# Recurrent layers of a four-layer encoder: channel tiles of 126 instead of 112, whole and halved gate blocks, gates of four tiles together

## The chip, the cores and the metric

One Trainium2 chip (trn2), of which one core is used. The kernel is one launch that runs a whole encoder trunk over 256 time steps. The metric is the device time of one execution in microseconds (us). Times are given as the median of three runs; the trace is of one further, profiled execution.

The engines have short names: PE is TensorE (PEld is its weight load, which overlaps it), DVE is VectorE, ACT is ScalarE, POOL is GpSimd, SP is SyncE, which here issues nearly all DMA transfers.

## The reference

Four layers of three sub-layers each: a token mixer, a cross-attention into 256 memory tokens, a squared-ReLU MLP, each followed by a layer norm. The mixers are, in order, recurrent, RWKV, chunked attention, recurrent. Only the recurrent mixer (layers 0 and 3) is touched. With 1344 channels in 16 blocks of 84:

```python
u = x @ w_in                                       # 256 x 1024 by 1024 x 2688
gate_branch = gelu(u[..., :1344])
xr = causal_depthwise_conv(u[..., 1344:], conv_w, conv_b)      # 4 taps
xb = xr.reshape(bsz, seq, 16, 84)
gates = einsum('bsnc,gncd->bsgnd', xb, gate_w) + gate_b        # two gates, block-diagonal
r, i = sigmoid(gates)
log_a = -8 * r * softplus(-lam)
a = exp(log_a)
b = sqrt(-expm1(2 * log_a)) * (i * xr)
h[t] = a[t] * h[t-1] + b[t]                        # along time, per channel
out = (h * gate_branch) @ w_out                    # 1344 x 1024
```

All of it is fp32.

## The kernel before

**Weights.** A large product is done three times, since each fp32 operand is split into a high part and a low remainder: `mm_piece` issues for each 128-row slice of a weight the matmuls high by high, low by high and high by low (L272, L273, L274). The weights come in a stream of chunks of two such slices: SP issues the load of a chunk into one of 4 buffers `wraw` (L105), ACT casts it to `whi` (L454), DVE forms `wlo` (L455), and after that `wlo` SP may issue the load that takes the buffer over, four chunks later. The splits run up to 7 chunks ahead of PE. All engines work through their instructions in the order in which the kernel writes them, and SP through its issues, so what stands ahead in a queue delays what stands behind it.

**The recurrent layer** (`lru`) holds its 1344 channels in 12 tiles of 112. Three tiles are four blocks of 84, so the gate products of three tiles (a *group*, `g`) are closed in themselves; a block that straddles two tiles makes 7 products of tile by tile (`GPAIRS`) for each gate. The steps stand in this order:

- `x_piece(0..2)`: the recurrent half of `w_in`, 448 columns each, and behind it, half a piece later, `conv(i)`: PE transposes to channels by time (L801), ACT scales (L807), DVE adds three taps (L811).
- `load_gw`: four loads of gate weights (343 KB, two groups) on SP's queue ahead of the remaining weight chunks, and the other four on ACT's queue, behind the sigmoids of groups 0 and 1 (L834). In layer 3 the two `mem_load` transfers (`kT`) follow them, in layer 0 they come after `x_piece(2)`.
- `gates(0)`, `conv(2)`, `gates(1)`, `gates(2)`, `gates(3)`: 14 fp32 matmuls of 256 columns a group (L847; each shows as two records), three times two sigmoids with a bias from `par` (L850, L851) and a tanh (L852), 256 wide, and one DVE product by the gate `i` (L853).
- `g_piece(0)` and `g_piece(1)`: the gelu half of `w_in`. Between their row halves stand `decay` (Exp, Square on ACT, L862, L864; DVE L865) and `scan` (Sqrt L868; DVE product L869 and a scan along time L871) of the four groups. The casts and the `wlo` of the next weight chunks stand in the same ACT and DVE queues, behind them. Exp, Square, Tanh and Sigmoid, Sqrt, and Gelu need ACT table loads when they change.
- In layer 0 `mem_split` (cast and remainder of `kT`: `memhi`, `memlo`), then `g_piece(2)` and the memory product L313, which fills PE between the groups of the last step.
- For each group PE transposes the gelu branch (L931), DVE multiplies (L934), and the result is split. `out_gemm` multiplies by `w_out`: 12 tiles by 2 column halves by 2 row halves by 3, 144 matmuls of 512 columns.

Of the kernel before, what the change touches and what calls it, by code (L numbers as in the profile page):

```python
# [16 lines left out]
T = 256  # L17
# [3 lines left out]
CT = 112  # L21
NT = DR // CT
GPAIRS = [(0, 0), (1, 0), (0, 1), (1, 1), (2, 1), (1, 2), (2, 2)]
# [42 lines left out]
class Stream:  # L66
# [46 lines left out]
    def _split(self):  # L113
        if self.ns >= len(self.plan):
            return
        k, i = self.k, self.ns
        while self.nd <= i:
            self._dma()
        _, _, p, f, whole = self.plan[i]
        raw = self.raw.pop(i)  # L120
        if whole:
            self.hl[i] = raw
            self.ns += 1
            return
        hi = k.hl_p.tile([128, 1024], F32R, name="whi", tag="whi")
        lo = k.hl_p.tile([128, 1024], F32R, name="wlo", tag="wlo")
        for c in self._cols(i, f):
            k.split(raw[:p, c], hi[:p, c], lo[:p, c])
        self.hl[i] = (hi, lo)
        self.ns += 1  # L130
        self._dma()
# [31 lines left out]
    def done(self, i):  # L163
# [9 lines left out]
        while self.ns < end and self.ns < i + self.hl_bufs:  # L173
            if any(self.plan[q][4] for q in range(i + 1, self.ns + 1)) and self.nd <= self.ns:
                break
            self._split()

# [54 lines left out]
class Kern:  # L232
# [20 lines left out]
    def mm_piece(self, acc, chunks, lhs, p, w, kpc=2, kt0=0, start=True, stop=True, last=False, near=None):  # L253
# [4 lines left out]
        for ci, c in enumerate(chunks):  # L258
            if not self.dry:
                wh, wl = self.st.hl[c]  # L260
                for k in range(kpc):
# [5 lines left out]
                    kt = kt0 + ci * kpc + k  # L267
                    a, b = lhs(kt)
                    ws = slice(k * w, (k + 1) * w)
# [393 lines left out]
    def out_gemm(self, name, idx, n, lhs, p):  # L663

        for nh in range(2):
            a = [self.acc(), self.acc()]
            parts = [range(n)] if n <= 4 else [range(n // 2), range(n // 2, n)]
            for part in parts:
                end = part is parts[-1]
                ch = [self.st.take(name, (*idx, nh, q), p, 1024) for q in part]  # L670
                last = end and nh == 1
                near = self.room(ch, self.next_ht()) if last else None
                for t in range(2):
                    self.mm_piece(a[t], ch, lhs[t], p, 512, kt0=2 * part[0], start=part[0] == 0, stop=end,
                                  last=t == 1 and not last, near=near if t else None)
# [104 lines left out]
    def lru(self, l, j):  # L780
        nc, tc = self.nc, self.tc
        with tc.tile_pool(name="lru", bufs=1, reuse_waits="tile") as p:
            par, cc = self.par[:, j], self.cc[:, j]
            gn = [p.tile([128, DR], F32, name=f"gn{t}") for t in range(2)]
            xc = [p.tile([CT, 3, T], F32, name="xc", tag="A", bufs=4) for _ in range(4)]
            nat = {}

            def x_piece(i):
                for t, a in self.gemm("lru_in", (j, 3 + i), 4, self.hT, 128, 448):
                    s = gn[t][:, 896:] if i == 2 else p.tile([128, 448], F32, name="xn", tag="CB"[i], bufs=4)  # L790
                    nc.scalar.copy(s, a[:, :448])
                    nat[i, t] = s
                    if i and t == 0:
                        conv(i - 1)

            def conv(i):
                for b in range(2):
                    ps = self.tp()
                    for q in range(2):
                        for t in range(2):  # L800
                            nc.tensor.transpose(ps[:CT, q * T + t * 128:q * T + t * 128 + 128],  # L801
                                                nat[i, t][:, (2 * b + q) * CT:(2 * b + q + 1) * CT], self.ident)
                    xy = []
                    for q in range(2):
                        c = 4 * i + 2 * b + q
                        x, y = ps[:CT, q * T:(q + 1) * T], xc[c // 3][:, c % 3, :]
                        nc.scalar.activation(y, x, AF.Identity, bias=par[:, c, 4:5], scale=par[:, c, 3:4])  # L807
                        xy.append((c, x, y))
                    for s in range(1, 4):
                        for c, x, y in xy:  # L810
                            nc.vector.scalar_tensor_tensor(  # L811
                                out=y[:, s:], in0=x[:, :T - s], scalar=par[:, c, 3 - s:4 - s], in1=y[:, s:],
                                op0=ALU.mult, op1=ALU.add)

            def g_piece(i, between=lambda t: None):
                accs = []
                for t, a in self.gemm("lru_in", (j, i), 4, self.hT, 128, 448):
# [4 lines left out]
            def gelu(i, accs):  # L822
                for t in range(2):
                    nc.scalar.activation(gn[t][:, i * 448:(i + 1) * 448], accs[t][:, :448], AF.Gelu_apprx_tanh)

            ra, th = [], []

            gws = []

            def load_gw(g, queue):  # L830
                gws.append([])
                for gate in range(2):
                    w = p.tile([CT, 7, CT], F32, name="gw", tag="gw", bufs=4)
                    queue.dma_start(w, self.I["lru_gw"][j, g, gate])  # L834
                    gws[g].append(w)

            def gates(g):
                gw = gws[g]
                r = p.tile([CT, 3, T], F32, name="ra", tag="B", bufs=4)
                h = p.tile([CT, 3, T], F32, name="th", tag="C", bufs=4)  # L840
                it = p.tile([CT, 3, T], F32, name="it", tag="tmp", bufs=2)
                for o in range(3):
                    ps = self.acc() if LV & 8 else self.mm()
                    ks = [(n, k) for n, (k, oo) in enumerate(GPAIRS) if oo == o]
                    for gate in range(2):
                        for n, k in ks:
                            nc.tensor.matmul(ps[:CT, gate * T:(gate + 1) * T], lhsT=gw[gate][:, n, :], rhs=xc[g][:, k, :],  # L847
                                             start=n == ks[0][0], stop=n == ks[-1][0])
                    c = 3 * g + o
                    nc.scalar.activation(r[:, o, :], ps[:CT, :T], AF.Sigmoid, bias=par[:, c, 6:7])  # L850
                    nc.scalar.activation(it[:, o, :], ps[:CT, T:], AF.Sigmoid, bias=par[:, c, 7:8])  # L851
                    nc.scalar.activation(h[:, o, :], r[:, o, :], AF.Tanh, scale=cc[:, c:c + 1])  # L852
                nc.vector.tensor_tensor(out=xc[g], in0=xc[g], in1=it, op=ALU.mult)  # L853
                ra.append(r)
                th.append(h)
                if g < 2:
                    load_gw(g + 2, nc.scalar)

            def decay(g):
                for o in range(3):  # L860
                    c = 3 * g + o
                    nc.scalar.activation(ra[g][:, o, :], ra[g][:, o, :], AF.Exp, scale=cc[:, c:c + 1])  # L862
                a2 = p.tile([CT, 3, T], F32, name="a2", tag="tmp", bufs=2)
                nc.scalar.activation(a2, ra[g], AF.Square)  # L864
                nc.vector.scalar_tensor_tensor(out=th[g], in0=a2, scalar=1.0, in1=th[g], op0=ALU.add, op1=ALU.mult)  # L865

            def scan(g):
                nc.scalar.activation(th[g], th[g], AF.Sqrt, scale=-1.0)  # L868
                nc.vector.tensor_tensor(out=th[g], in0=th[g], in1=xc[g], op=ALU.mult)  # L869
                for o in range(3):  # L870
                    nc.vector.tensor_tensor_scan(xc[g][:, o, :], ra[g][:, o, :], th[g][:, o, :], 0.0, ALU.mult, ALU.add)  # L871

            x_piece(0)
            for g in range(2):
# [6 lines left out]
            V = LV  # L881
            if V & 1:
                gates(0)
# [3 lines left out]
            if not V & 1:  # L887
                gates(0)
            if V & 2:
                gates(1)  # L890
                conv(2)
            else:
                conv(2)
                gates(1)
            if V & 4:
                decay(0)
                decay(1)
            gates(2)
            gates(3)
            if V & 4:  # L900
                def bt(t):
                    if t == 0:
                        decay(2)
                        decay(3)
                    else:
                        scan(0)
                g0 = g_piece(0, bt)
            else:
                g0 = g_piece(0, lambda t: (decay(2 * t), decay(2 * t + 1)))
            for t in range(2):  # L910
                nc.vector.tensor_copy(gn[t][:, :448], g0[t][:, :448])
            if V & 4:
                g1 = g_piece(1, lambda t: (scan(1), scan(2)) if t == 0 else (scan(3),))
            else:
                g1 = g_piece(1, lambda t: (scan(2 * t), scan(2 * t + 1)))
# [6 lines left out]
            hi, lo = [], []  # L922
            for g in range(4):
                hi.append(p.tile([CT, 3, T], F32R, name="yhi", tag="B", bufs=4))
                lo.append(p.tile([CT, 3, T], F32R, name="ylo", tag="C", bufs=4))
                for o0, n in ((0, 2), (2, 1)):
                    ps = self.tp()
                    for q in range(n):
                        for t in range(2):
                            c = 3 * g + o0 + q  # L930
                            nc.tensor.transpose(ps[:CT, q * T + t * 128:q * T + t * 128 + 128],  # L931
                                                gn[t][:, c * CT:(c + 1) * CT], self.ident)
                    y = xc[g][:, o0:o0 + n, :]
# [1014 lines left out]
```

## Time and profile before

| | before |
|---|---|
| median of three runs | 1807.71 us (1806.71 to 1808.3) |
| profiled execution, its own time | 1807.5 us |
| its span in the trace | 1805.7 us |
| PE busy | 1742.7 us (97% of the span) |
| DVE busy | 1252.2 us (69%) |
| ACT busy | 872.7 us (48%) |
| granted TensorE clock, mean | 0.991 |

The span is what the trace covers, from the first to the last instruction; the time of the same execution is 1.8 us longer, which lies around the span. A busy share is an average over twelve sub-layers with different limits. In the two recurrent layers PE has gaps of some microseconds, which the views below show one by one.

### The profile page before, as it was taken

Reading aid. Unit: us, or ns where it says so; the run is one execution under the profiler, and the core shown is the slowest. Engines: PE = TensorE matmul, PEld = TensorE weight load, DVE = VectorE, ACT = ScalarE, POOL = GpSimd, SP = SyncE. Lnnn points to the kernel's source line nnn. Section 1 sums busy time; section 2 is a strip of 40 time slices with the busy share of each in tenths; the row PEclk is TensorE's granted clock in tenths of the full one; section 3 lists DMA queues with packets and bytes.
Section 4 is the critical chain, followed back from the end, with each engine's and each line's share of the span. In section 5 each row is a group of like instructions: output and inputs, shape, how many; then the busy total and the mean of one; then the engine's idle time right before and its main releaser. Section 6 shows DMA issues by size and latency. Waiting matters only on the chain.

```text
span 1805.7 us, 25667 instructions
## 1 busy us (share of the span) xinstructions
PE 1742.7 (97%) x10032; PEld 1459.8 (81%) x10032; DVE 1252.2 (69%) x1809; ACT 872.7 (48%) x1338; POOL 50.3 (3%) x64
## 2 busy tenths in 40 slices
PE   8989999999999889999999999999999999999998
PEld 7778988888677556888887888888888887988886
DVE  6487676667578798786667567876667677677665
ACT  6664644444554133544444453634444674545442
POOL 2000000000000001000000000000000000000000
PEclk9999999999999999999999999999999999999999
DMA  7455456556241324355555724545555645636552
GB/s 240 134 177 182 165 182 221 186 199 208 93 144 48 118 83 130 139 205 191 188 190 184 260 88 140 168 169 199 187 187 175 182 139 161 217 119 230 187 187 94
DMA packets 92928, 302.39 MB, mean 167 GB/s; under 512 B 11907, under 2 KB 19587, under 8 KB 92677
## 3 DMA queue, kind: packets, MB, share of 16 engines
q1 hardware_dynamic: 91780, 297.92, 49.7%
q10 hardware_dynamic: 1024, 2.81, 0.6%
q8 instruction: 79, 1.29, 0.3%
q14 instruction: 45, 0.36, 0.1%
HBM read 299.65 MB, written 1.05 MB: 167 GB/s over the span
## 4 chain that ended last, share of the span: by engine, by line
PE 80%; DVE 9%; DMA 5%; ACT 4%; issue 2%; SPq 1%; POOL 0%; DVEq 0%; ACTq 0%
PE acc L274 12%; PE acc L272 12%; PE acc L273 12%; PE tp L293 5%; PE mm L293 5%; PE acc L293 4%; PE acc L516 4%; PE acc L313 4%; PE tp L294 3%; PE mm L294 3%; PE mm L847 2%; PE acc L191 2%; PE tp L351 2%; DMA wraw<-in_lru_in 2%; PE acc L294 2%; DVE wlo L455 2%
## 5 line engine op out<-in xcount | busy, mean ns | idle before, releaser
L455 DVE TENSOR_TENSOR wlo<-wraw,whi 128x1024 fp32r<-128x1024 f32 (+3 forms) x505 | 593.8, 1206 | 136.8 <-ACT whi L454 125.0
L454 ACT CAST whi<-wraw 128x1024 fp32r<-128x1024 f32 (+3 forms) x505 | 508.3, 1039 | 219.2 <-PE acc L274 151.4
L272 PE MATMUL acc<-whi,ahi 128*128 128x512 f32 x512 | 200.3, 391 | 0.0
L274 PE MATMUL acc<-whi,alo 128*128 128x512 f32 x512 | 199.7, 390 | 0.0
L273 PE MATMUL acc<-wlo,ahi 128*128 128x512 f32 x512 | 199.4, 389 | 0.0
L272 PE MATMUL acc<-whi,ht 128*128 128x448 f32 (+1 forms) x368 | 143.2, 389 | 5.3 <-ACT whi L454 5.3
L273 PE MATMUL acc<-wlo,ht 128*128 128x448 f32 (+1 forms) x368 | 141.2, 384 | 3.5 <-DVE wlo L455 3.5
L274 PE MATMUL acc<-whi,ht 128*128 128x448 f32 (+1 forms) x368 | 141.3, 384 | 1.6 <-DVE ht L355 1.6
L293 PE MATMUL tp<-ht,whi 128*128 128x512 f32 x384 | 136.7, 398 | 0.0
L293 PE MATMUL mm<-ht,whi 128*128 128x512 f32 x384 | 136.5, 398 | 0.0
L293 PE MATMUL acc<-ht,whi 128*128 128x512 f32 x352 | 127.1, 402 | 2.3 <-DVE qkT L992 2.3
L274 PEld LDWEIGHTS acc<-whi,alo 128*128 128x128 f32 x512 | 96.1, 188 | 20.9
L272 PEld LDWEIGHTS acc<-whi,ahi 128*128 128x128 f32 x512 | 96.1, 188 | 20.2
L273 PEld LDWEIGHTS acc<-wlo,ahi 128*128 128x128 f32 x512 | 96.2, 188 | 19.2
L294 PE MATMUL tp<-ht,wlo 128*128 128x256 f32 x384 | 107.9, 281 | 0.0
L294 PE MATMUL mm<-ht,wlo 128*128 128x256 f32 x384 | 107.8, 281 | 0.0
L294 PE MATMUL acc<-ht,wlo 128*128 128x256 f32 x352 | 99.3, 282 | 0.0
L739 DVE TENSOR_TENSOR rel<-mm,rel 128x256 f32<-128x256 f32 x48 | 18.6, 425 | 110.4 <-ACT rel L738 110.4
L743 ACT CAST ahi<-rel 128x512 fp32r<-128x512 f32 x56 | 34.8, 621 | 110.1 <-DVE rel L742 110.1
L293 PEld LDWEIGHTS tp<-ht,whi 128*128 128x128 f32 x384 | 72.2, 188 | 18.0
L293 PEld LDWEIGHTS mm<-ht,whi 128*128 128x128 f32 x384 | 72.1, 188 | 17.6
L272 PEld LDWEIGHTS acc<-whi,ht 128*128 128x128 f32 x368 | 70.2, 191 | 16.9 <-ACT whi L454 5.9
(387 smaller groups left out, 3378.3 us busy)
## 6 DMA issues: line engine op xcount, KB each, us to landing
wraw<-in_w SPq DMA_DIRECT2D x256, 512.0 KB, 4.5
wraw<-in_w_kv SPq DMA_DIRECT2D x64, 512.0 KB, 4.5
wraw<-in_lru_in SPq DMA_DIRECT2D x47, 448.0 KB, 4.6
wraw<-in_w_q SPq DMA_DIRECT2D x32, 512.0 KB, 4.3
wraw<-in_w_co SPq DMA_DIRECT2D x32, 512.0 KB, 4.6
wraw<-in_ca_qkv SPq DMA_DIRECT2D x24, 512.0 KB, 4.6
wraw<-in_lru_out SPq DMA_DIRECT2D x24, 448.0 KB, 5.1
ln_gt<-in_ln_g SPq DMA_DIRECT2D x12, 512.0 KB, 5.9
```

Source lines behind the costliest of these rows:

```text
L191: return f(*a, **k)
L272: nc.tensor.matmul(acc[:, :w], lhsT=a, rhs=wh[:p, ws], start=s, stop=False)
L273: nc.tensor.matmul(acc[:, :w], lhsT=a, rhs=wl[:p, ws], start=False, stop=False)
L274: nc.tensor.matmul(acc[:, :w], lhsT=b, rhs=wh[:p, ws], start=False, stop=e)
L293: self.nc.tensor.matmul(four, lhsT=wh[:, ws], rhs=xy, start=s, stop=False)
L294: self.nc.tensor.matmul(four[:, :2], lhsT=wl[:, ws], rhs=x, start=False, stop=e)
L313: self.nc.tensor.matmul(a, lhsT=w[:, ws], rhs=v, start=s and i == 0, stop=e and i == 2)
L351: self.nc.tensor.transpose(dst_ps[:n, j * p:(j + 1) * p], s, self.ident[:p, :p])
L454: self.nc.scalar.copy(hi, src)
L455: self.nc.vector.tensor_tensor(out=lo, in0=src, in1=hi.bitcast(F32), op=ALU.subtract)
L516: nc.tensor.matmul(a, lhsT=u, rhs=w[:, ws], start=s, stop=e)
L847: nc.tensor.matmul(ps[:CT, gate * T:(gate + 1) * T], lhsT=gw[gate][:, n, :], rhs=xc[g][:, k, :], start=n == ks[0][0], stop=n == ks[-1][0])
```

## The change

The host now reorders the channels (of `w_in`, `w_out`, the convolution, the gates) so that five triples of blocks a, b, c fill two tiles of 126 each: the first half of c, all of a and 64 channels of b, then the second half of c and the rest of b. A sixteenth block is a tile of 84 alone. With that order each tile needs one product with its own 126 by 126 block, and each pair of tiles two products with 42 rows of the other tile, which lie at rows 0 to 41 and 64 to 105. So per gate and layer there are 11 whole and 10 half products, 42 matmuls in both gates. The groups are 4, 4 and 3 tiles.

```diff
-CT = 112
-NT = DR // CT
-GPAIRS = [(0, 0), (1, 0), (0, 1), (1, 1), (2, 1), (1, 2), (2, 2)]
+CT = 126
+NT = 11
+LB = 84
+LW = 504, 504, 336
...
-            xc = [p.tile([CT, 3, T], F32, name="xc", tag="A", bufs=4) for _ in range(4)]
+            xc = [p.tile([CT + 1, n, T], F32, name="xc", tag=f"A{g}") for g, n in enumerate(tiles)]
+            for x in xc:
+                nc.gpsimd.memset(x, 1.0)
...
+                    for o, ps in enumerate(pss):
+                        nc.tensor.matmul(ps[:CT, gs], lhsT=gw[:CT + 1, gate, o * CT:(o + 1) * CT], rhs=xc[g][:, o, :],
+                                         start=True, stop=o == n - 1 and n % 2 == 1)
+                    for b in range(n // 2):
+                        w = slice((n + b) * CT, (n + b + 1) * CT)
+                        for u in range(2):
+                            a = slice(64 * u, 64 * u + 42)
+                            nc.tensor.matmul(pss[2 * b + 1 - u][:CT, gs], lhsT=gw[a, gate, w], rhs=xc[g][a, 2 * b + u, :],
+                                             start=False, stop=True)
+                for o, ps in enumerate(pss):
+                    nc.scalar.activation(r[:, :, o, :], ps[:CT, :].rearrange("p (g t) -> p g t", g=2), AF.Sigmoid)
+                v = r[:, 0, :n, :]
+                nc.vector.tensor_tensor(out=v, in0=v, in1=cc[:, 4 * g:4 * g + n].unsqueeze(2).to_broadcast([CT, n, T]), op=ALU.mult)
+                x = xc[g][:CT, :n, :]
+                nc.vector.tensor_tensor(out=x, in0=x, in1=r[:, 1, :n, :], op=ALU.mult)
...
+            def tanh(g):
+                nc.scalar.activation(ri[g][:, 1], ri[g][:, 0], AF.Tanh)
...
+                a2 = p.tile([CT, 4, T], F32, name="a2", tag="C")[:, :n, :]
+                nc.scalar.activation(a, a, AF.Exp)
+                nc.scalar.activation(a2, a, AF.Square)
...
-            for g in range(2):
+            for g in range(3):
                 load_gw(g, nc.sync)
...
+            gates(0)
+            conv(2)
+            tanh(0)
+            if l == 0:
+                self.mem_split()
+            gates(1)
+            tanh(1)
             gates(2)
-            gates(3)
...
+            tanh(2)
+            g0 = g_piece(0, lambda t: (decay(0), decay(1)) if t == 0 else decay(2))
...
+            g1 = g_piece(1, lambda t: (scan(0), scan(1)) if t == 0 else scan(2))
             gelu(0, gn)
             gelu(1, g1)
-            if l == 0:
-                self.mem_split()
...
-            self.out_gemm("lru_out", (j,), 6, [lhs(0), lhs(1)], CT)
+            self.out_gemm("lru_out", (j,), 6, [lhs(0), lhs(1)], CT, tail=("lru_out2", LB))
```

What else follows from it: the bias of the gates is a row of the gate weights (row 126), met by a row of ones in `xc`, which POOL sets; the two sigmoids of a tile are one instruction of 512 columns; the factor of the decay is multiplied once by DVE (L888), so that Tanh and Exp are one instruction for a whole group; Square has one buffer instead of two. The tanh writes over gate `i`, so it stands behind the product L890. The six pieces of `w_in` are 504, 504 and 336 columns wide. The 11 row tiles of `w_out` make ten chunks of 128 rows (two rows are padding) and two chunks of 96 by 512 (12 rows are padding). The gate weights come in three loads a layer, all on SP's queue: 128 rows by 1512 (774 KB) twice and 128 by 1008 (516 KB). `out_gemm` has 132 matmuls.

On PE in layer 0, behind `x_piece(2)`, the gates of groups 0 to 3 with the transposes of `conv(2)` between stood so before (`x14` counts matmuls in a row that read alike; `gn_178` and `gn_179` are the two row halves of the last piece):

```order
L847 MATMUL mm<-xc,gw 112x256 x14
L801 MATMUL tp<-ident,gn_178 112x128
L801 MATMUL tp<-ident,gn_179 112x128
...
L847 MATMUL mm<-xc,gw 112x256 x42
L272 MATMUL acc<-whi,ht 128x448
```

In the change the same place, groups 0 and 1 (L877 is a whole product, L883 a half one; `mm` and `acc` are banks of PSUM, two tiles of each):

```order
L877 MATMUL mm<-xc,gw 126x256 x2
L877 MATMUL acc<-xc,gw 126x256 x2
L883 MATMUL mm<-xc,gw 126x256 x2
L883 MATMUL acc<-xc,gw 126x256 x2
...
L834 MATMUL tp<-ident,gn_178 126x128
...
L834 MATMUL tp<-ident,gn_179 84x128
L877 MATMUL acc<-xc,gw 126x256 x2
L877 MATMUL mm<-xc,gw 126x256 x2
L883 MATMUL acc<-xc,gw 126x256 x2
L883 MATMUL mm<-xc,gw 126x256 x2
```

The gates of four tiles now stand whole, half, whole, half, once for each gate, so PE changes between full and half tiles six times a layer and back.

On ACT in layer 0, what stood between the gates of groups 0 and 1 before, and the place of the memory's casts far behind (after Gelu):

```order
L852 ACTIVATE th<-ra,cc 112x256
L834 DMA gw<-in_lru_gw 112x784 x2
L807 ACTIVATE xc<-tp,par 112x256 x4
L850 ACTIVATE ra<-mm,par 112x256
...
L824 ACTIVATE gn_179<-acc 128x448
L454 CAST memhi<-kT 128x1024 x2
L454 CAST whi<-wraw 128x1024 x2
```

And in the change (L886 sigmoid, L894 tanh, L900 Exp, L901 Square):

```order
L886 ACTIVATE ri<-acc 126x2x256 x2
L840 ACTIVATE xc<-tp,par 126x256 x2
L840 ACTIVATE xc<-tp,par 84x256
L894 ACTIVATE ri<-ri 126x1024
L471 CAST memhi<-kT 128x1024 x2
L886 ACTIVATE ri<-acc 126x2x256 x2
L886 ACTIVATE ri<-mm 126x2x256 x2
L894 ACTIVATE ri<-ri 126x1024
L886 ACTIVATE ri<-acc 126x2x256 x2
L886 ACTIVATE ri<-mm 126x2x256
L894 ACTIVATE ri<-ri 126x768
L900 ACT_TABLE_LOAD
```

The casts `memhi` have moved ahead of the sigmoids of groups 1 and 2, and no DMA is issued on ACT any more.

On SP in layer 0, around the gate weights before:

```order
L105 DMA wraw<-in_lru_in 128x896 x6
L834 DMA gw<-in_lru_gw 112x784 x4
L105 DMA wraw<-in_lru_in 128x896 x8
L442 DMA kT<-in_memT 128x8x128 x2
```

and in the change:

```order
L106 DMA wraw<-in_lru_in 128x672 x4
L865 DMA gw<-in_lru_gw 128x1512 x2
L865 DMA gw<-in_lru_gw 128x2x504
L106 DMA wraw<-in_lru_in 128x1008 x8
L459 DMA kT<-in_memT 128x8x128 x2
```

All gate weights of the layer now stand ahead of the eight chunks and of `kT`.

## Rows read from the trace of the kernel before

**Rows 1.** Page: span, and busy time by engine.

```profile
span 1805.7 us, 25667 instructions
PE 1742.7 (97%) x10032; PEld 1459.8 (81%) x10032; DVE 1252.2 (69%) x1809; ACT 872.7 (48%) x1338; POOL 50.3 (3%) x64
```

**Rows 2.** Chain of waits, layer 0, 40 to 130 us: start, us, what.

```profile
43.54 6.06 PE mm L847 x28
...
60.68 14.30 PE mm L847 x52
...
92.51 1.86 DVE xc L871 x3
...
97.11 4.26 DVE wlo L455 x4
...
102.25 11.72 DMA wraw<-in_lru_out
...
116.37 0.61 DVE xc L934
```

**Rows 3.** The same chain, layer 3, 1376 to 1500 us.

```profile
1407.55 8.83 DMA wraw<-in_lru_in
...
1420.05 2.39 PE mm L847 x8
...
1424.15 18.58 PE mm L847 x84
...
1464.86 3.13 DVE wlo L455 x3
...
1479.14 0.61 DVE xc L934
```

**Rows 4.** Waits of PE, first 30 to 130 us, then 1379 to 1500 us.

```profile
PE tp L931 <- DVE xc L934: 3.5, 1, 3.5
PE mm L847 <- DMA gw<-in_lru_gw: 3.1, 2, 1.6
PE acc L313 <- DVE memlo L455: 2.9, 1, 2.9
PE acc L273 <- DVE wlo L455: 1.1, 1, 1.1
...
PE mm L847 <- ACT it L851: 2.6, 1, 2.6
```

**Rows 5.** Window in the gates, layer 0: us, PE busy, granted clock, DMA share, GB/s.

```profile
60.70:66.40 5.70, 5.70 (x14) 0.50 0.27 68
```

**Rows 6.** Timeline of PE, matmuls on 64-row tiles, in the RWKV and attention layers.

```profile
561.89 2.06 PE L191 MATMUL acc<-ar,ht 64*128 64x128 f32 x32
...
1048.12 0.28 PE L313 MATMUL acc<-memhi,whi 128*128 128x256 f32 x1
1048.33 1.13 PE L1019 MATMUL mm<-qkT,qkT 64*128 64x256 f32 x4
1049.39 0.39 PE L313 MATMUL acc<-memlo,whi 128*128 128x256 f32 x1
```

**Rows 7.** Window of `out_gemm`, layer 0, columns as in group 5.

```profile
128.00:160.00 32.00, 31.99 (x141) 1.00 0.68 204
```

**Rows 8.** Groups of instructions, 40 to 135 us: busy us, mean ns.

```profile
L862 ACT ACT_TABLE_LOAD x1 | 1.3, 1283 | 0.0
L868 ACT ACTIVATE th<-th 112x768 f32<-112x768 f32 x4 | 3.2, 839 | 0.0
L853 DVE TENSOR_TENSOR xc<-xc,it 112x768 f32<-112x768 f32 x4 | 3.8, 958 | 19.4 <-ACT it L851 16.9 <-PE tp L801 2.5
```

**Rows 9.** Transfers: loads of `kT` in layer 0, and a window's rate (last number, GB/s).

```profile
L442 SPq DMA_DIRECT2D kT<-in_memT x2: 661/732/802, 46.4 to 47.1; - x2
...
DMA to landing us min/median/max: 6.5/7.3/8.1
...
21.30:36.10 14.80, 14.80 (x79) 13.59 (x77) 9.07 (x18) 7.29 (x11) 5.42 (x16) 1.00 0.93 283
```

More of the change, by code (lines that the diff above doesn't have):

```diff
@@ L251, in chunks, with mm_piece @@
         return [self.st.take(name, (*idx, q), p, f) for q in range(n)]
-    def mm_piece(self, acc, chunks, lhs, p, w, kpc=2, kt0=0, start=True, stop=True, last=False, near=None):
+    def mm_piece(self, acc, chunks, lhs, p, w, kpc=2, kt0=0, start=True, stop=True, last=False, near=None, tail=None):
         nc = self.nc
@@ L260, in mm_piece @@
                 wh, wl = self.st.hl[c]
+                if tail and ci == n - 1:
+                    p, kpc, ci0 = tail, 1, 2 * ci
+                else:
+                    ci0 = ci * kpc
                 for k in range(kpc):
@@ L669, in out_gemm @@
                 end = part is parts[-1]
-                ch = [self.st.take(name, (*idx, nh, q), p, 1024) for q in part]
+                short = tail is not None and end
+                ch = [self.st.take(name, (*idx, nh, q), 128 if tail else p, 1024) for q in part[:len(part) - short]]
+                if short:
+                    ch.append(self.st.take(tail[0], (*idx, nh), 96, 512))
                 last = end and nh == 1
@@ L674, in out_gemm @@
                     self.mm_piece(a[t], ch, lhs[t], p, 512, kt0=2 * part[0], start=part[0] == 0, stop=end,
-                                  last=t == 1 and not last, near=near if t else None)
+                                  last=t == 1 and not last, near=near if t else None, tail=tail[1] if short else None)
                     if last and t == 0:
@@ L837, in gates @@
[L837 to L857, printed above, removed]
@@ L859, in decay @@
-            def decay(g):
[L860 to L865, printed above, removed]
-            def scan(g):
[L868 to L871, printed above, removed]
+                m = tiles[g] + tiles[g] // 2
@@ new lines, in load_gw, with gates @@
+                w = p.tile([128, 2, m * CT], F32, name="gw", tag=f"gw{g}")
+                queue.dma_start(w, self.I["lru_gw"][j, g, :, :, :m * CT])
+                gws.append(w)
+            def gates(g):
+                n, gw = tiles[g], gws[g]
+                r = p.tile([CT, 2, n, T], F32, name="ri", tag=f"B{g}")
+                ms = [self.mm, self.mm, self.acc, self.acc]
+                pss = [bank() for bank in (ms if g == 0 else ms[::-1])[:n]]
+                for gate in range(2):
+                    gs = slice(gate * T, (gate + 1) * T)
+                    for o, ps in enumerate(pss):
[13 more added lines that the diff above has]
+                nc.vector.tensor_tensor(out=x, in0=x, in1=r[:, 1, :n, :], op=ALU.mult)
+                ri.append(r)
@@ L927, in lru @@
+            for g in range(3):
+                n = tiles[g]
+                hl.append(p.tile([CT, 2, n, T], F32R, name="yhl", tag=f"B{g}"))
+                for b in range(2):
+                    cs = range(4 * g + 2 * b, min(4 * g + 2 * b + 2, NT))
                     ps = self.tp()
-                    for q in range(n):
+                    m = wide(cs[0])
+                    for q, c in enumerate(cs):
                         for t in range(2):
-                            c = 3 * g + o0 + q
-                            nc.tensor.transpose(ps[:CT, q * T + t * 128:q * T + t * 128 + 128],
-                                                gn[t][:, c * CT:(c + 1) * CT], self.ident)
```

162 lines of the change are left out of this document (85 added, 77 removed).

## The prediction

> **What bounds the kernel now.** The page comes first: PE is busy for 1742.7 of 1805.7 us, DVE for 1252.2 [rows 1]. The rest of PE is 63 us in twelve sub-layers, so the change can gain in two ways only: less work on PE, or fewer of the gaps that lie in the two recurrent layers. The chain of waits says which of the two counts where. In layer 0 it runs through the gate matmuls (28 records in 6.06 us, 0.216 each, two records a matmul, then 52 in 14.30) [rows 2], then leaves PE: Exp, Sqrt, products and scans on ACT and DVE, the `wlo` casts that stand behind the scans (97.11), four chunks of `w_out` that SP may issue only then (landing at 102.25 + 11.72 = 113.97), their cast and remainder, and the product with the gelu branch that stands behind those on DVE (116.37) [rows 2]. Layer 3 shows the same with the `wlo` at 1464.86 and the product at 1479.14; ahead of its gates there is a chunk of `w_in` that lands at 1407.55 + 8.83 = 1416.38, and a stop of the gates at 1420.05 [rows 3]. The waits of PE say what the gaps are worth: 3.5, 3.1, 2.9, 1.1 us in layer 0, and 2.6 in layer 3 at the gates [rows 4]. So the reader should see a layer that is bound by PE up to the end of the gates, and from there until `out_gemm` by a chain whose length PE has little part in.
>
> **PE's work.** Before, 56 gate matmuls a layer, two records each: 112 x 0.216 = 24.2 us [rows 2]. After, 22 whole ones take 44 x 0.216 = 9.5, and the row count of 127 instead of 112 costs nothing, since a record's time goes by its 256 columns. The 20 halves are the open price. In the RWKV layer 32 records on 64-row tiles that alternate between the two row halves end in 2.06 us for 128 columns, 0.064 each [rows 6]; for 256 columns that is 0.13 each, 40 records in 5.2, and 4.3 if only the steady rate of 0.108 a record counts. In the attention layer four records of 256 columns in one row half take 1.13, with both changes of tile size inside [rows 6]; at the plain 0.216 the 20 halves would be 40 x 0.216 = 8.6. The kernel alternates rows 0 to 41 and 64 to 105 and writes different banks, which is nearest to the RWKV row: I take 4.3. Changing tile size: from 1048.12 to 1048.33 is 0.21, where a record of that line takes about 0.12 in a run, and 1048.33 to 1049.39 is 1.06 for four records of 0.216, 0.2 over [rows 6]; 0.28 for there and back, six times a layer, 1.7. Together 15.5, a gain of 8.7 us.
>
> [...]
>
> `out_gemm` has 12 matmuls fewer, 32.00 / 141 = 0.227 each [rows 7], 2.7 us a layer. The pieces of `w_in` have the same columns in all (288 x 448 = 192 x 504 + 96 x 336), so they count as nothing, and so do four transposes fewer; between nothing and a gain of 1 us together. Sum on PE: 11.4 a layer, 23 in both. That would be the whole gain if nothing else moved.
>
> **What the gates' start does, layer 0.** Ahead of the last chunks of the recurrent half now stand all three gate loads, 2.06 MB instead of 1.40 in four. At the 283 GB/s of that stretch [rows 9] 0.66 MB are 2.3 us. The gates began at 43.54; the later chunks bring between 0 and 2.3, and as the last piece is now 336 wide instead of 448, so less is behind the last arrival, I take 1.4: 44.8 to 44.9. [...] The new wait is the memory's casts. They stand on ACT ahead of the sigmoids of group 1; the second `kT` load was issued at 47.1 and landed 8.1 later, at 55.2 [rows 9]; with the 2.3 that SP is late 57.4, and the cast behind it ends at 58.4. Behind it on ACT are four sigmoids of some 0.5 us, which free the bank that the third tile of group 2 needs at 60.0, and 2.9 us of its products follow: the gates end at 63.0, not at 60.68 + 14.30 = 75.0 (their last record starts before that, at 74.6). 11.6 us earlier.
>
> **The chain behind the gates.** It was 74.6 to 98.2 (97.11 and the first of four `wlo`), 23.6; in layer 3 1442.4 to 1465.9, 23.5 [rows 2, 3]. What is in it now: the tanh of group 1 that is not yet done 0.65, three sigmoids 1.6, two DVE products 1.9, tanh of group 2 0.85, table load 1.28, Exp and Square of two groups of four 4.4, four weight casts 3.4, Exp and Square of the third 1.7, table load 1.28, Sqrt 1.06, two groups of product and four scans 7.2, the first `wlo` 0.8. The durations are those of 112x768 on ACT, 0.84, and on DVE, 0.96 [rows 8], by 4/3 where a group has four tiles, and scans of 1.86/3 = 0.62 [rows 2]. Sum 26.1: the chain is longer by 2.5 than it was, as the `wlo` now wait for eight scans and not six, and as one instruction of 1024 must end where three of 256 could be followed by others. So `wlo` is ready at 63.0 + 26.1 = 89.1, with half a microsecond for one buffer of `a2` 89.7, against 98.2: 8.5 of 11.6 arrive. PE has caught up and waits there 2.5 to 3 us, where it waited 1.1 [rows 4].
>
> From `wlo` on, the transfers set the time: 98.2 to 116.4 before, 18.2. Eight loads lie in it, four chunks of `w_out` and two each for the residual and the norm, 4.2 MB with the chunks of the change, 15 us at 283 GB/s; the padding of the four chunks (112 to 128 rows, 0.26 MB) is 0.9 of them. So the product with the gelu branch starts at 89.7 + 18.2 + 0.9 = 108.8, 7.6 earlier, and PE, whose work in that stretch is unchanged, waits for it for some 8 us in place of the 3.5 and 2.9 [rows 4]. With 2.7 of `out_gemm` behind it, layer 0 gains 10.3.
>
> **Layer 3.** Here `kT` and the gate loads are ahead of the chunk that lands at 1416.38. 0.66 MB, and 0.1 MB of wider chunks, make it 2.7 later, 1419.1; the copy behind its cast and the transposes of `conv(2)` follow at 1420.5, where the wait of 2.6 was (1420.05), and PE stands about as long; the eight records behind that wait took 2.39 where 8 x 0.216 are 1.7 [rows 3], and I leave that loss as it is. The gates end at 1433.5 instead of 1442.4, 8.9 earlier; the chain of 26.1 gives `wlo` at 1459.6, 6.3 earlier. Behind it only one group of scans is left to be done before the product, not two (one product and three scans, some 2 us of DVE): 1470.6 instead of 1479.1. With 2.7, layer 3 gains 11.1.
>
> **Covered.** The POOL memsets of `xc`, 0.8 each by POOL's mean (50.3 / 64) [rows 1], lie beside 14 us of transfers; without that cover they cost 2.4 in layer 0. The new product on DVE (L888) and the padding of rows cost PE nothing where DVE waits anyway; the first is in the chain's sum.
>
> **Sum.** 10.3 + 11.1 = 21.4. The profiled execution took 1807.5, its span 1805.7 and 1.8 around it that I leave as they are: 1786.1, and 1786.3 by the median of 1807.7, which is 0.2 above. I say 1786.
>
> **The rivals.**
> A, as above, with each term within its bounds: 1780 to 1792, chance 0.5.
> B, the halves run one after another: 4.3 more on PE a layer, of which layer 0's wait for casts hides 2; 21.4 - 6.6 is 14.8, 1793. The RWKV row speaks against it. 0.1.
> C, the chain of ACT and DVE gives back most of the gates: it is 33 and not 26 us. Then layer 0 gains 3 and layer 3 gains 4, 1800. For it speaks that ACT has bigger instructions and one `a2`; against it that ACT has fewer of them. 0.12.
> D, transfers: all gate loads ahead of the weights cost 4 us more a layer, as SP's queue is in use at 0.93 [rows 9] and every later chunk moves with it. 1794. 0.12.
> E, the stops at the gates vanish and nothing takes their place, while the waits of the chain stay as they are: 23 of PE, 3.1 + 2.6 [rows 4] and the 3 of the clock, 31.7, 1776. 0.08.
> F, slower: PE stops oftener and for shorter runs, and its clock falls each time as it did behind 58 us. A fall is 3 us; there are about five stops a layer in the sum above (convolution, cast, chunk, product, group). All ten would be 30 against 21.4, 1816; it decides from the eighth. Against it: a stop of 2.6 at 1420.05 was followed by eight slow records and then by 84 in 18.58, 0.221 each [rows 3], so a stop of that size alone costs less than 1. 0.04. [...]
> G, C and D together leave nothing: 1807. 0.04.
>
> A difference of 0.2% (3.6 us) is about what a measurement of this kernel can tell from no change. Faster by more than that are A to E, 0.92; same G, 0.04; slower F, 0.04. From 1776 to 1800 hold A, B, C and D, 0.84, and with their overlap a little of E.
>
> **What would show it.** Gate records: 84 a layer, ending near 63 and 1433; the halves in pairs at about 0.22 a pair. A wait of PE for `memhi` or a sigmoid of group 1 near 58. The first `wlo` behind the scans near 89.7 and 1459.6, and the first product with the gelu branch near 108.8 and 1470.6, with a wait of PE of 8 us ahead of it in layer 0. `out_gemm` of 132 records at 0.227. I am wrong if PE has no wait there (then E), if the gates of layer 0 start after 47 (D), or if the `wlo` come more than 30 us behind the gates (C).

## The result and the profile after

The changed kernel took 1786.16 us (median of four, 1781.64 to 1787.01), the kernel before beside it 1807.23. The ratio is 0.9878 with a 95% interval of 0.986 to 0.9895: 1.2% faster, and on the forecast of 1786. The steps behind the forecast were less exact than their sum, as the rows show: that the time came out on the number is luck in part.

The page, span and busy time by engine [rows 1]:

```profile
span 1784.4 us, 25405 instructions
...
PE 1723.6 (97%) x9944; PEld 1432.5 (80%) x9944; DVE 1248.9 (70%) x1795; ACT 852.4 (48%) x1268; POOL 55.5 (3%) x70
```

PE is busy for 19.1 us less, a time in which the slow stretches of its clock count too (the mean granted clock is 0.987, before 0.991), and the span is 21.3 shorter. The chain of waits in layer 0, 40 to 125 us [rows 2]:

```profile
47.95 8.33 DMA kT<-in_memT
...
58.87 1.10 PE mm L877 x2
...
63.98 1.18 PE acc L883 x4
...
89.91 3.79 DVE wlo L472 x4
...
94.26 9.96 DMA wraw<-in_lru_out
...
106.62 0.61 DVE xc L953
```

and in layer 3, 1370 to 1490 us [rows 3]:

```profile
1400.98 7.91 DMA wraw<-in_lru_in
...
1423.50 1.59 ACT ri L886 x3
...
1448.23 3.80 DVE wlo L472 x4
...
1460.17 0.61 DVE xc L953
```

The links are those that were forecast: `kT`, the casts, the gates' end, a chain of ACT and DVE to the first `wlo`, the loads of `w_out`, the product with the gelu branch (L953). The waits of PE, 5 to 125 us and then 1360 to 1490 [rows 4]:

```profile
PE tp L950 <- DVE xc L953: 5.8, 1, 5.8
PE acc L289 <- ACT whi L471: 5.5, 2, 5.2
PE mm L877 <- ACT ri L886: 2.6, 1, 2.6
PE acc L290 <- DVE wlo L472: 1.4, 2, 0.9
...
PE acc L290 <- DVE wlo L472: 1.6, 1, 1.6
PE tp L950 <- DVE xc L953: 1.1, 1, 1.1
...
PE mm L877 <- DVE xc L844: 0.7, 1, 0.7
```

(5.2 of the second row is the start of the program, which before had too.) The stops for gate loads are gone, one of 2.6 for a sigmoid behind the memory's casts is new, and the wait for the product has grown to 5.8. PE's timeline in the gates of layer 0 [rows 5, 6]:

```profile
42.70 1.03 PE L877 MATMUL mm<-xc,gw 127*126 127x256 f32 x4
43.56 1.03 PE L877 MATMUL acc<-xc,gw 127*126 127x256 f32 x4
44.52 0.70 PE L883 MATMUL mm<-xc,gw 42*126 42x256 f32 x4
45.05 0.60 PE L883 MATMUL acc<-xc,gw 42*126 42x256 f32 x4
45.58 1.13 PE L877 MATMUL mm<-xc,gw 127*126 127x256 f32 x4
...
58.87 1.10 PE L877 MATMUL mm<-xc,gw 127*126 127x256 f32 x2 [2.60 <-ACT ri L886]
59.91 1.22 PE L883 MATMUL acc<-xc,gw 42*126 42x256 f32 x4
61.06 2.07 PE L877 MATMUL acc<-xc,gw 127*126 127x256 f32 x4
```

Eight records of half products, 44.52 to 45.58, take 1.06 with a change of tile size, 0.13 each, where a record of a whole product takes 0.216: they run in pairs. From 58.87 on the same work takes twice as long (four half records from 59.91 to 61.06, 1.15 for the 0.53 of 44.52 to 45.05), and the window of that stretch says why (us, PE busy, granted clock, DMA share, GB/s):

```profile
58.80:65.30 6.50, 6.43 (x17) 0.52 0.00 0
```

**Where the time went.** Transposes that are alike in both programs show it layer by layer. Behind the recurrent part of layer 0 they stand at 160.56 before and 148.24 after, 12.3 earlier; ahead of layer 3 at 1377.55 and 1370.33, only 7.2 earlier; the spans end 21.3 apart. So layer 0 gained 12.3 (forecast 10.3), layer 3 gained 14.1 (forecast 11.1), and what lies between, in which nothing was edited, lost 5.1 (forecast 0).

### The profile page after: what moved, and what is told of

Read it like the earlier page. It is cut to its first block, busy times and chain, and to the rows that moved or that the text cites. A ratio compares the mean times of both kernels' runs of the same rounds, so it can differ in the third digit from the quotient of the medians.

```text
span 1784.4 us, 25405 instructions
## 1 busy us (share of the span) xinstructions
PE 1723.6 (97%) x9944; PEld 1432.5 (80%) x9944; DVE 1248.9 (70%) x1795; ACT 852.4 (48%) x1268; POOL 55.5 (3%) x70
## 4 chain that ended last, share of the span: by engine, by line
PE 80%; DVE 10%; ACT 4%; DMA 3%; issue 2%; POOL 0%; SPq 0%; DVEq 0%; ACTq 0%
PE acc L291 12%; PE acc L290 12%; PE acc L289 12%; PE tp L310 5%; PE mm L310 5%; PE acc L310 4%; PE acc L533 4%; PE acc L330 4%; PE tp L311 3%; PE mm L311 3%; PE acc L203 2%; PE tp L368 2%; DVE wlo L472 2%; PE acc L311 2%; PE mm L502 1%
## 5 line engine op out<-in xcount | busy, mean ns | idle before, releaser
L472 DVE TENSOR_TENSOR wlo<-wraw,whi 128x1024 fp32r<-128x1024 f32 (+4 forms) x505 | 591.8, 1203 | 145.8 <-ACT whi L471 134.0
L471 ACT CAST whi<-wraw 128x1024 fp32r<-128x1024 f32 (+4 forms) x505 | 507.3, 1035 | 220.4 <-PE acc L291 147.5
L289 PE MATMUL acc<-whi,ht 128*128 128x512 f32 (+2 forms) x368 | 143.3, 389 | 5.5 <-ACT whi L471 5.5
L290 PE MATMUL acc<-wlo,ht 128*128 128x512 f32 (+2 forms) x368 | 141.5, 384 | 3.9 <-DVE wlo L472 3.9
L291 PE MATMUL acc<-whi,ht 128*128 128x512 f32 (+2 forms) x368 | 141.5, 385 | 1.7 <-DVE ht L372 1.7
L290 PEld LDWEIGHTS acc<-wlo,ahi 128*128 128x128 f32 x512 | 96.2, 188 | 19.2
```

The lines of the kernel that those rows point to most:

```text
L289: nc.tensor.matmul(acc[:, :w], lhsT=a, rhs=wh[:p, ws], start=s, stop=False)
L290: nc.tensor.matmul(acc[:, :w], lhsT=a, rhs=wl[:p, ws], start=False, stop=False)
L291: nc.tensor.matmul(acc[:, :w], lhsT=b, rhs=wh[:p, ws], start=False, stop=e)
L471: self.nc.scalar.copy(hi, src)
L472: self.nc.vector.tensor_tensor(out=lo, in0=src, in1=hi.bitcast(F32), op=ALU.subtract)
```

## The experiments

Each was timed in rounds beside the kernel before. The table gives the time, the ratio with its interval, and what the profiled execution gained (minus) or lost in us against the first profile of before, found from the same PE instructions in both traces: in layer 0, between the end of its recurrent part and layer 3 (nothing edited), and in layer 3. It goes by other instructions than the transposes above, which moves a figure by 0.1.

| kernel | median us | ratio, 95% | layer 0 | between | layer 3 |
|---|---|---|---|---|---|
| changed | 1786.16 | 0.9878 (0.986 to 0.9895) | -12.2 | +5.0 | -14.1 |
| changed, again | 1785.05 | 0.9877 (0.9854 to 0.9899) | -11.2 | +2.0 | -14.7 |
| before, again | 1804.88 | 1.0004 (0.9986 to 1.0022) | +1.3 | +3.6 | +0.4 |
| before, loads of 128 rows | 1797.74 | 0.9951 (0.9932 to 0.9969) | -7.1 | +1.6 | -3.1 |
| no padding at all | 1931.36 | 1.0691 (1.0677 to 1.0706) | | | |
| `w_out` unpadded | 1790.06 | 0.9903 (0.9881 to 0.9926) | -8.0 | +1.6 | -11.2 |
| third gate load on ACT | 1789.08 | 0.9898 (0.9879 to 0.9916) | -8.5 | +1.6 | -11.2 |
| late casts | 1779.44 | 0.985 (0.9836 to 0.9863) | -16.4 | +2.0 | -13.5 |
| one scan | 1783.66 | 0.9865 (0.9845 to 0.9885) | -14.6 | +3.6 | -12.1 |
| late casts, one scan in layer 0 | 1776.58 | 0.9833 (0.9815 to 0.985) | -20.0 | +2.1 | -13.6 |
| casts between scans | 1776.67 | 0.983 (0.9807 to 0.9854) | -19.2 | -2.3 | -13.0 |

**1 and 2. Both kernels once more, nothing edited.**

> The changed kernel once more, nothing edited. What is asked: its four runs lie between 1781.6 and 1787.0, and its profile shows three falls of the clock (1.7 us of work each) in layers 1 to 3 that the profile of before doesn't have. Theory one (the falls are chance: where the short gaps of the RWKV layer meet the throttle): the runs spread again over some 5 us, 1781 to 1787, and the falls in this profile stand at other places or in other number. Theory two (the change puts them there, by its shift of the program in time): the profile has them again near 448, 598, 608 and 1148 us, and all runs lie within 1 us of 1786.

> The kernel of before once more, nothing edited. The four profiles of changed kernels so far all have two falls of the clock near 596 to 612 (RWKV layer, behind waits of 1.0 and 1.9 us) that cost 1.4 to 1.8 us each, and one more of these near 450, 650 or 1148; the one profile of before has none of them. Theory one (which waits of the untouched layers end in a slow stretch is chance of each execution): this profile has falls near 607 to 617 or at other places that the first one lacks, and its time differs from 1807.5 by the like of 1.5 us a fall. Theory two (the falls come with the changed kernel): none near 607 to 617, layers 1 and 2 take what they took, and the two profiles of before agree within 0.5 us there.

Theory one held. The second profile of before has slow stretches of the clock near 460, 620, 664, 678, 992 and 1160 us (each with a window of 2 us at a granted clock of 0.50) that the first, with its own near 674, 752 and 990, mostly lacks, and is 3.6 us longer between the two recurrent layers. The changed kernel alone gave 1778.64 to 1790.62 in five runs. The 5 us lost in untouched layers were chance of one execution: in the second profile they were 2.0, and over the profiles in the table the changed kernel and its variants lie between -2.3 and +5.0 there, the kernel before and its variant between 0 and +3.6. That profile of the changed kernel again had falls near 600 and 610 (0.50 from 598 to 600 and from 608 to 610), so some places are favoured, but the runs do not agree within 1 us as theory two asked.

**3. Before, with loads of 128 rows.** The products still read 112 rows.

```diff
-                ch = [self.st.take(name, (*idx, nh, q), p, 1024) for q in part]
+                ch = [self.st.take(name, (*idx, nh, q), 128, 1024) for q in part]
...
-                    w = p.tile([CT, 7, CT], F32, name="gw", tag="gw", bufs=4)
+                    w = p.tile([128, 7, CT], F32, name="gw", tag="gw", bufs=4)
...
```

> The kernel of before with nothing edited but the rows of two kinds of loads: w_out chunks and gate weights come as 128 rows in place of 112 (16 rows of zeros, 14% more bytes); the products still read 112 rows. Theory rows (112 rows use the 16 engines badly): from 22 to 34 us the rate goes from 290 to 340 GB/s or more, in the stretch ahead of the product with the gelu branch from 292 to 340 or more; the stops of the gates at 58 and 60.7 shrink to 1 us or less each, the product comes some 1 us earlier than 116.4; 1 to 5 us faster. Rival (the rates of the changed kernel came from its longer rows of 4 and 6 KB): the rates stay near 290, the bytes make the product 0.9 us later and the gates' stops some 0.3 each longer; 0 to 2 us slower.

8 us faster by medians, with 14% more bytes in those loads; more than the 1 to 5 of the theory. A window of the stretch with its first gate loads and some chunks of `w_in` (us, granted clock, DMA share, GB/s):

```profile
21.50:31.00 9.50, 1.00 0.99 360
```

Before, the like stretch had

```profile
22.80:32.40 9.60, 1.00 1.02 299
```

and the changed kernel

```profile
22.80:32.40 9.60, 1.00 1.00 370
```

So the rate rises by a fifth with a DMA share near 1 in all three. From its chain of waits in layer 0:

```profile
57.63 13.18 PE mm L847 x52
...
97.85 10.54 DMA wraw<-in_lru_out
...
110.80 0.61 DVE xc L934
```

One of the two stops of the gates has gone, the 52 records end at 70.81 and not 74.98 [rows 2], and the product comes 5.6 earlier. Some 1.7 of that lie ahead of the gates, which begin at 41.71 for 43.38; in the second profile of before they began at 42.13, so part of it is chance. The padding of both loads is thus worth some 7 us in layer 0 and 3 in layer 3 of the old kernel, where I had put that of `w_out` down as a loss of 0.9. Which of the two loads brings how much was not parted. Nor was the gain of the change: 8 us of the 21 can be had in the old kernel by padding alone, and no run has the new tiles with the old rows, so how the 21 divide between less work on PE and earlier transfers is not shown.

**4. The changed kernel without padded rows, and with `w_out` alone unpadded.** The first loads 127 rows of gate weights and 126 or 84 of `w_out`, the second has 128 for the gates.

```diff
-                queue.dma_start(w, self.I["lru_gw"][j, g, :, :, :m * CT])
+                queue.dma_start(w[:CT + 1], self.I["lru_gw"][j, g, :CT + 1, :, :m * CT])
...
-                ch = [self.st.take(name, (*idx, nh, q), 128 if tail else p, 1024) for q in part[:len(part) - short]]
+                ch = [self.st.take(name, (*idx, nh, q), p, 1024) for q in part[:len(part) - short]]
...
```

> The changed kernel without padded rows: w_out chunks of 126 rows and of 84, gate weights of 127 rows. What is disputed: the transfers ran at 370 GB/s at the gate loads and 346 in the stretch ahead of the product with the gelu branch, where before they had 290 and 292, so my 1.4 and 2.7 us for the larger gate loads were not paid. Theory rows (the number of rows sets how well the 16 engines are used): both stretches fall back to some 290 to 310 GB/s, the product with the gelu branch comes 1.5 to 3 us later, the gates' start up to 2 later, time 1788 to 1792. Rival (longer rows of 4 and 6 KB made it): the rates stay at 340 or more, and the time stays within 1 us.

Far outside what either expected, 145 us slower than the changed kernel. A window in layer 0 (us, granted clock, DMA share, GB/s):

```profile
40.00:60.00 20.00, 0.54 0.06 26
```

and the waits of PE there:

```profile
PE tp L834 <- ACT xn L823: 72.5, 1, 72.5
```

26 GB/s at a DMA share of 0.06, which is that of one engine of 16, while PE stands for 72.5 us in layer 0 alone. So not 290 to 310 but a tenth of that, and one more run had to part the two loads.

> The changed kernel with the rows of the w_out chunks as they are needed, 126 and 84, while the gate loads keep 128 (with 127 rows these moved at 26 GB/s, a DMA share of 0.06, one engine of 16). Asked is whether the 145 us of the kernel without any padding were the gate loads alone. Theory (rows set how many engines a transfer gets; 126 and 84 still divide among 14 of them): the w_out stretch of layer 0 loses 10 to 15% of its rate, the product with the gelu branch comes 0.5 to 1.5 us later, out_gemm has a wait or two for chunks; 0 to 4 us slower than the changed kernel, 1785 to 1790. Rival (126 rows are as bad as 127): more than 20 us slower.

Some 4 us slower than the changed kernel by the medians, in ranges that overlap (1784.77 to 1791.71). The last load ahead of the product takes

```profile
96.06 12.35 DMA wraw<-in_lru_out
```

in place of 9.96. By the table 126 rows cost 3 to 4 us a recurrent layer, but in layer 0 some 1.4 of it can't come from `w_out`, which is loaded later: PE waited 2.3 for a `wlo` at 36.2, the granted clock from 36 to 40 was 0.57, and the gates began at 44.08. What is left is 2 to 3 us in layer 0 and about 3 in layer 3, where PE's wait for the product rose from 1.1 to 3.1. The 127 of the gate loads cost nearly all of the 145 in both layers. The traces show shares of the engines' time, not a cause: besides the 0.06 of 127 rows, 0.88 at 326 GB/s from 173 to 176 us of the run without padding, where chunks of `w_out` with 126 rows stand in line, and 1.02 at 394 GB/s from 100.2 to 104.2 us of the changed kernel, whose chunks have 128. Of 16 engines 0.06 is one and 0.88 is 14, which are estimates from the shares. With 112 rows the share is no lower, 1.02, and the rate was still 299 against 360 GB/s (experiment 3); what sets it, no run shows.

**5. The third gate load where the late ones stood before.**

```diff
-            for g in range(3):
+            for g in range(2):
                 load_gw(g, nc.sync)
...
             gates(0)
+            load_gw(2, nc.scalar)
```

> The changed kernel with the gate load of group 2 (516 KB) on ACT's queue behind the sigmoids of group 0, as the later loads stood before. My prediction's term (loads ahead of the weight chunks make the gates start later, 0.66 MB for 1.4 us in layer 0 and 2.7 in layer 3): the gates start 1 us earlier in layer 0 and the chunk behind kT lands 1.5 us earlier in layer 3; if group 2 then waits for its load, that is below 1 us. Rival (the chunks are hidden behind PE's own work there): the gates start where they did, within 0.3 us of 42.7 in layer 0, and nothing is gained; and a stop for the load behind the sigmoids may cost 1 to 3 us in layer 0.

The rival held: the gates start at 42.88, no earlier than 42.70, and a stop of 2.25 for the load is added to one of 1.68 for the sigmoid. In layer 3 the chunk behind `kT` lands at 1409.09, which is 1416.0 by before's clock (6.9 added) and 0.1 from where the changed kernel has it. 3 to 4 us slower by the medians, in ranges that overlap, and by 3.7 and 2.9 in the two recurrent layers of its profile against the first one of the changed kernel. The term of my sum for loads ahead of the weights was worth nothing.

**6. The memory's casts back behind Gelu.** `mem_split` of layer 0 moves from behind `tanh(0)` to behind `gelu(1, g1)`.

```diff
             tanh(0)
-            if l == 0:
-                self.mem_split()
...
             gelu(1, g1)
+            if l == 0:
+                self.mem_split()
```

> The changed kernel with the memory's cast and remainder of layer 0 back where they stood before (behind the second Gelu). My theory (layer 0 is PE up to the gates' end, then a chain of fixed length): the wait of 2.6 at 58.9 goes, the slow clock from 58 to 70 goes with it (some 2.5), the gates end near 60 in place of 65, and the first product with the gelu branch comes 2 to 5 us earlier than 107.2; a wait for memlo comes in front of the memory product, below 3. Layer 0 gains 2 to 4, time 1782 to 1784. Rival (the casts cost the same wherever they stand): the 2.1 us of ACT and 2.4 of DVE move behind the scans and come before the cast and the remainder of the w_out chunks, the memory product waits for memlo as it did before, and the time stays within 1 us of the changed kernel's.

6 us faster than the changed kernel by the medians, and 4 to 5 in layer 0, more than the theory's 2 to 4, with both effects that it named: the wait of 2.6 for the sigmoid is gone (0.3 for the convolution is left), and so is the slow stretch at the gates (the granted clock is 1.00 from 54 to 70 us). The wait for `memlo` that it expected didn't come. Its chain:

```profile
85.08 3.79 DVE wlo L472 x4
...
89.48 10.23 DMA wraw<-in_lru_out
...
102.12 0.61 DVE xc L953
```

Every link is 4.5 to 4.8 earlier. The move of the casts, one of the edits of the change, was a loss of 4 to 5 us in layer 0.

**7. One group of scans between the row halves.**

```diff
-            g1 = g_piece(1, lambda t: (scan(0), scan(1)) if t == 0 else scan(2))
+            g1 = g_piece(1, lambda t: scan(0) if t == 0 else (scan(1), scan(2)))
```

> The changed kernel, but between the row halves of the second gelu piece stands only the scan of group 0; those of groups 1 and 2 come behind the second row half. My theory (the weight remainders stand behind eight scans on DVE and the loads of w_out behind those): the first remainder comes 3.6 us earlier in both recurrent layers (near 86.3 in place of 89.9), the wait of PE there goes, the product with the gelu branch comes 2 to 3.6 earlier in layer 0 and 1 to 2 in layer 3; together 3 to 5, time 1781 to 1783. Rival (transfers or ACT set the product's time, not the remainders): the remainders come earlier, but the loads wait for PE to give their buffers free or the product waits for its own scans, and the time stays within 1 us of the changed kernel's.

In layer 0 the theory held to the step: the load of `w_out` is issued at 90.41 and the product comes at

```profile
102.96 0.61 DVE xc L953
```

3.7 earlier. Layer 3 lost 2 instead: there the `wlo` of `w_out` now stand behind seven scans on DVE, right ahead of the product, and the wait for it rose from 1.1 to 2.1, with a slow stretch of the clock behind it (0.50 from 1458 to 1460). By time alone the kernel can't be told from the changed one (1776.89 to 1786.89).

**8. Both in layer 0, layer 3 as the changed kernel has it.**

> The changed kernel with the two edits that shortened layer 0 together, in layer 0 alone: the memory's cast and remainder behind the second Gelu, and only the scan of group 0 between the row halves of the second gelu piece. Layer 3 is left as the changed kernel has it, since one scan there made it 2 us longer. Theory (a chain: what is taken off it anywhere comes out at its end, until PE's own work is the bound): layer 0 gains 4 from the one and 2.5 to 3.5 from the other, the first product comes near 98 to 99 in place of 106.6, layer 0 is 18 to 19.5 shorter than before's, time 1774 to 1778. Rival (PE's own work or the memory's remainder is next): the product's wait is used up, layer 0 stays within 1 us of the one with the late casts alone, time 1778 to 1781.

1776.58, 1.7% faster than before, and its slowest run (1777.49) is below all nine of the changed kernel (1778.64 and more). It beats both kernels. Layer 0 gained 20.0. The wait for the product has gone, and PE's largest wait behind the gates is

```profile
PE acc L330 <- DVE memlo L472: 3.6, 1, 3.6
```

**9. The casts between the row halves, ahead of the scan of group 1.**

> The kernel with late casts and one scan in layer 0, but the memory's cast and remainder stand between the row halves of the second gelu piece, ahead of the scan of group 1. In the kernel without this edit PE waits 3.6 us for memlo ahead of the memory product and no longer for the product with the gelu branch. Theory (each link of the chain is worth what it is late): memlo is ready 6 us earlier, the wait of 3.6 goes, the next limit is the cast and remainder of the w_out chunks some 1 us behind it, so layer 0 gains 2 to 3.6 more, 1773 to 1775. Rival (the casts only change places: ACT has the casts of the weights behind them): the w_out chunks or the scans are later by the 2.1 to 2.4 us, and layer 0 stays within 1 us, 1776 to 1777.

The rival held. The wait for `memlo` went, and waits of 2.7 for the product and 1.7 for a weight remainder took its place; layer 0 is 0.8 longer, the time the same. (Some 0.3 of the 0.8 lie ahead of the edit, where PE waited 2.2 for a remainder at 35.5 and the gates began at 43.42 for 43.10.) What stays open is whether layer 0 has a next link that is worth taking.

## Why the prediction was right, point by point

**Its sum** was right partly because errors of both signs met, and that is luck. By the two profiles the recurrent layers gained 26 where 21.4 was forecast, and slow stretches of the clock in untouched layers gave back 5 and 2.

**PE's work.** The halves run side by side, as the RWKV row had it: B is out. A record of 127 rows takes what one of 112 took: four stand from 42.70 to 43.56, 0.215 each, for 0.216 [rows 2]. 40 half records and their changes of tile size were put at 6.0 a layer, with the 0.108 of a half record an estimate, half of 0.216; four visits of eight records at 1.06 and two of four at 0.63 (1420.63 to 1421.26 in layer 3) are 5.5. All gates of a layer at full clock are 15.8, four times 2.88 (42.70 to 45.58) and twice 2.12, for 15.5. Rival E is out, since waits took the place of those removed.

**The gates' start** is the step that failed. "At the 283 GB/s of that stretch" priced 0.66 MB at 1.4 us in layer 0 and 2.7 in layer 3. The gates began at 42.70 for the forecast 44.9 (42.43 in the second profile), where the two profiles of before have 43.38 and 42.13, so nothing was lost that is clear of chance. In layer 3 the chunk behind the gate loads landed at 1408.89, which is 1416.1 by before's clock (7.2 added), 3.0 ahead of the forecast 1419.1. Two things were wrong in the price. The rate was one: at 370 GB/s 2.06 MB are 5.6 us and at 299 GB/s 1.40 MB are 4.7 (experiment 3), so 0.9 of the 2.3 is left. The wait was the other: what is left did not set the gates' start, which stayed where it was with 0.5 MB fewer ahead (experiment 5). The trace of before had the hint. I took the 283 GB/s at a DMA share of 0.93 for the most there was, and it has a window with more at a like share (us, PE busy, granted clock, DMA share, GB/s):

```profile
100.00:110.00 10.00, 7.11 (x42) 1.00 0.95 340
```

D is out with it.

**The wait for the memory's casts** was foreseen in its place: `kT` landed at 56.28 for 57.4, and PE waited 2.6, up to 58.87 for 60.0. Its price was not: the clock fell behind it, to 0.52, and the gates ended at 65.2 for 63.0. The 3 us that E and F give one fall are 52 records in 14.30 less 52 x 0.216 [rows 2], in part at the clock of [rows 5]; here 6.43 us of work at 0.52 make it 3.1, an estimate. That is what rival F described, at one place, and experiment 6 took it away. That F as a whole would decide was wrong: the slow stretches of whole executions are as many in before, again.

**The chain of ACT and DVE** was put at 26.1 from the gates' end to the first `wlo`; 65.2 to 89.91 and a quarter of 3.79 are 25.7. C is out. In layer 3 it is 1423.5 to 1449.2, again 25.7.

**From `wlo` to the product** 18.2 and 0.9 for padding were forecast, and 15.8 measured (90.9 to 106.6): the padded chunks land sooner, not later. PE's wait was 5.8 for 8, and the 2.5 to 3 that it should have stood at the first `wlo` were nothing in the first profile and 1.6 in the second. The product came at 106.6 for 108.8, and layer 0 gained 2 more than forecast.

**Layer 3** gained 3 more, since its chunk was not late (above): the gates end at 1430.7 by before's clock for 1433.5, and each link behind it is as much ahead. (The forecast's own 8.5 and 2.7 make 11.2 there, not 11.1.)

**Covered work.** No wait of PE for POOL or for L888 shows in its list, as forecast. But the POOL memsets of `xc` were not covered in layer 0. They stand on POOL behind its work on the factor of the decay, begin at 28.65, and ACT's scaling for the convolution waits for the first of them:

```profile
ACT xc L840 <- POOL xc L812: 1.9, 1, 1.9
```

All eight profiles of kernels with the new tiles and padded gate loads have this wait, 1.4 to 3.3 us. The taps of the convolution on DVE stand behind it, then the `wlo` for which PE waits 0.9 at 36.34. No run has the memsets earlier, so what they cost is not shown. The padding of rows, forecast as nothing for PE and a loss for the transfers, is another of the covered edits that was wrong: alone it gave the old kernel 7 us in layer 0 (experiment 3).

## What to carry to other kernels

Before a load's bytes are priced, look at its number of rows: 128 rows with zeros beat 112 without (360 GB/s against 299), and 127 moved at less than a tenth of the rate (26 GB/s). Where a chain ends in loads that are issued only after work on another engine, what stands in that engine's queue ahead of the release sets the loads' time; moving two groups of instructions there brought 8 us more in layer 0. And a forecast that lands on the number is checked step by step: here a gain and a loss were both missed.

## What the runs showed of the hardware

- A transfer of 127 rows ran at 26 GB/s and a DMA share of 0.06. The stretch with the gate loads had 360 GB/s at 0.99 with 128 rows, and 299 at 1.02 with 112. Chunks of 126 rows ran at 326 GB/s and 0.88, of 128 rows at 394 and 1.02.
- Half products of 42 rows at rows 0 and 64, into different banks, ran in pairs: 0.13 us a record with one change of tile size in eight, against 0.216 for a record of a whole product.
- A wait of 2.6 us of PE between the gates was followed by 6.5 us at a granted clock of 0.52. All five traces of such kernels with a wait of 1.7 to 3.0 us there had 0.50 to 0.60 in that window, and the three without had 1.00. In layers without any edit, such stretches came and went between executions of one kernel, and runs of the kernel before lay between 1799.68 and 1813.27.
